# Seven block products instead of eight for the gates and ups of the second feed-forward, with one shared pool of equal tiles

## Chip, cores and metric

The kernel runs on one core of a Trainium2 chip. The metric is device time in microseconds (us) for one launch, the median of several runs. The engines are TensorE (PE, with its weight loads as PEld), VectorE (DVE), ScalarE (ACT), GpSimd (POOL) and SyncE (SP), whose queue issues nearly all the transfers.

## Reference

One layer of a hybrid bidirectional encoder over 768 real tokens (512 of one sequence, 256 of another) and 16 meta tokens, with rows of 1024 features:

```
h = h + 0.5 * swiglu(rmsnorm(h), ffn1 ...)                 # first feed-forward
u = rmsnorm(h);  proj = u @ w_in                           # q, k, v, z, xbc, dt
h = h + concat[diff_attention(q,k,v), ssd_mixer(z,xbc,dt)] @ w_out
h = h + 0.5 * swiglu(rmsnorm(h), ffn2 ...)                 # second feed-forward
y = rmsnorm(h), meta tokens dropped
swiglu(u, wg, wu, wd) = (silu(u @ wg) * (u @ wu)) @ wd      # wg, wu: 1024 x 2816, wd: 2816 x 1024
```

## Kernel before

All of h lives on chip with the features on the partitions: eight tiles of 128 features by the tokens. A float32 product is made of three products in float32r: each operand is split into a large part and a rest (`split`, L145: ScalarE casts the large part, VectorE subtracts it from the source for the rest), and `mm3` (L242) issues large x large, rest x large and large x rest (L246, L247, L248). `dense` runs `mm3` over the eight (or four) blocks of 128 features.

Weights come as blocks of 512 x 256 (512 KB) in the order of `plan`. `Weights.dma` loads a block into one of two buffers `wr`, `Weights.split` splits it into one of four buffers `wh` (large parts) and four `wl` (rests), and `done`, called after each product, allows the next split once a product's weights are used up (`NHL = 4` split blocks at a time). A raw buffer is free again when both parts of its block are made.

The second feed-forward, `ffn(2, ...)`, works on pairs of 128 hidden features, 11 pairs in all, in two halves of 384 tokens. For each pair, `gate_up` makes the gates (silu on ScalarE, L381) and then the ups (multiplied with the gates on VectorE, L390, and split for the last product): 2 weights x 2 rows of 128 x 2 halves, each one `dense` of eight blocks, 24 matmuls of 384 columns. `down` adds the product of a group of pairs with its part of `wd` to h (L410). The groups are `BOUNDS = [0, 1, 3, 5, 7, 9, 11]`: the first holds one pair, the others two, and the down product of a group is issued after the first pair of the next group.

The norm ahead of it, `nf = Norm(...)`, follows the last part of the output projection (`o_unit`, part 3), half by half. Its `chain` is a generator on the agenda: each `done` runs one step of it, and `nf.get(hf)` issues all that is left before the first product of that half. It makes 1/rms (`tok_rstd`), spreads it over the partitions (`bcast`), and for each of eight blocks scales h (L317) and splits it into rows `u`.

Memory on chip is in tagged pools: `u`, 16 tiles of 784 columns for split rows; `w3`, 16 tiles of 804 columns; `w4`, 15 tiles of 1056 columns; the weights' buffers; small ones. PSUM has three tags: `mm` and `x`, two banks each, and `S`, two pairs of banks. A tile is given a buffer of its tag when one is free. In the mixer stage each row of z and of the queries is gathered in a `w3` tile (written by L1041, two halves) and stored to DRAM by L1044.

Of the kernel before, what the change touches and what calls it, by code (L numbers as in the profile page):

```python
# [14 lines left out]
P = 128  # L15
# [32 lines left out]
def body(tc, x_prompt, x_sample, meta_tokens, ffn1_norm_w, ffn1_w_gate, ffn1_w_up, ffn1_w_down,  # L48
# [10 lines left out]
    up = top.enter_context(tc.tile_pool(name="up", bufs=1))  # L59
    wk = top.enter_context(tc.tile_pool(name="wk", bufs=1))  # L60
    sm = top.enter_context(tc.tile_pool(name="sm", bufs=1))
# [4 lines left out]
    def row_u():  # L66
        return up.tile([P, T1], F32R, tag="u", name="rowu", bufs=16)

    def w4(n=1056, dt=F32):
        return wk.tile([P, 1056], dt, tag="w4", name="w4", bufs=15)[:, :n]  # L70

    def w3(n=XW + 1, dt=F32):
        return wk.tile([P, XW + 1], dt, tag="w3", name="w3", bufs=16)[:, :n]
# [23 lines left out]
    # Silu's table, before the first data are there  # L97
# [10 lines left out]
    plan = []  # L108

    def plan_w8(key, src, c0, ncol=256):  # L110
        plan.extend(((key, 0), src, 0, 4, c0, ncol) if i == 0 else ((key, 4), src, 4, 4, c0, ncol) for i in range(2))
# [10 lines left out]
    def plan_down(f, wd, g):  # L122
        k0, k1 = 2 * BOUNDS[g], 2 * BOUNDS[g + 1]
        for cp in range(KD // 2):
            plan.append(((f, "d", g, cp), wd, k0, k1 - k0, cp * 256, 256))
# [15 lines left out]
    for part, k0 in enumerate(OUT_K):  # L141
        for cp in range(4):
            plan.append((("o", part, cp), w_out0, k0, 4, 256 * cp, 256))
    plan_ffn(2, ffn2_w_gate[0], ffn2_w_up[0], ffn2_w_down[0])
# [13 lines left out]
    NRAW, NHL = 2, 4  # L158

    class Weights:  # L160
        raw, ready = {}, {}
        n_dma = n_split = n_got = n_free = 0

        def dma(self):
            if self.n_dma >= len(plan):
                return
            key, src, k0, nk, c0, ncol = plan[self.n_dma]
# [11 lines left out]
        def split(self):  # L179
            j = self.n_split  # L180
            while self.n_dma <= j:
                self.dma()
            key, _, _, nk, _, ncol = plan[j]
            raw = self.raw.pop(j)
            hi = wp.tile([P, 4, 256], F32R, tag="wh", name="wh", bufs=NHL)
            lo = wp.tile([P, 4, 256], F32R, tag="wl", name="wl", bufs=NHL)
            ins = split(hi[:, :nk, :ncol], lo[:, :nk, :ncol], raw[:, :nk, :ncol])
            if ncol == 32:
                V.tensor_copy(hi[:, :nk, 32:64], lo[:, :nk, :32].bitcast(F32))
            self.ready[key] = [(hi[:, i, :], lo[:, i, :]) for i in range(nk)]  # L190
            self.n_split += 1
            while self.n_dma < max(self.n_split, 2) + NRAW and self.n_dma < len(plan):
                self.dma()
            return ins

        def pump(self, most=1):
            while most and self.n_split < min(len(plan), self.n_free + NHL):
# [3 lines left out]
        def get(self, key):  # L201
            assert plan[self.n_got][0] == key, (plan[self.n_got][0], key)
# [20 lines left out]
    def done(free=0):  # L223
        """A dense product has been issued: the next weights, then a step of what goes on beside it."""
# [6 lines left out]
    def complete(gen):  # L231
        """All of gen is issued by now."""
# [11 lines left out]
    def mm3(ps, a, b, start, stop):  # L244
        (ah, al), (bh, bl) = a, b
        nc.tensor.matmul(ps, ah, bh, start=start, stop=False)  # L246
        nc.tensor.matmul(ps, al, bh, start=False, stop=False)  # L247
        last_mm[0] = nc.tensor.matmul(ps, ah, bl, start=False, stop=stop)  # L248
# [9 lines left out]
    def rsqrt(v, name):  # L258
        """1/sqrt of a small tile of positive numbers: a first guess from the bits, then Newton's steps."""
# [11 lines left out]
    def diags(r, tiles):  # L271
        """diag(r[:n, j]) for each of tiles (j, n)."""
# [5 lines left out]
    def bcast(dst, dg, tiles):  # L278
        """dst's columns get the diagonals of dg, the same on each partition."""
# [7 lines left out]
    def add_sq(h, m, sums):  # L287
        """The squares of row m; the last row's are added to the others' sum by tok_rstd."""
        if m == 0:
            sums.append(w3(h.shape[-1]))  # L290
            S.activation(sums[0], h, AF.Square)
        elif m < KD - 1:
            sq = w3(h.shape[-1])
            S.activation(sq, h, AF.Square)
            G.tensor_tensor(sums[0], sums[0], sq, ALU.add)
        else:
            sums.append(w3(h.shape[-1]))
# [14 lines left out]
    def make_u(h, w, r_bc, c0, c1, u, ks):  # L312
        """u = the normed rows, columns c0..c1, split; r_bc starts at c0."""
# [9 lines left out]
    class Norm:  # L323
        """Follows the last additions to h, one half of the tokens at a time."""
# [14 lines left out]
        def get(self, hf):  # L339
            """The split rows, good for a half (or, without one, whole)."""  # L340
# [19 lines left out]
    def ffn(f, h, halves, u, after, first=None, last=None, rms=None):  # L360
        """first, last: other parts of the tokens for the first gates and the last sums; rms: 1/rms, if u is without."""
# [77 lines left out]

    h_d = dram.tile([KD, P, T2], F32, name="h_d")  # L440
# [27 lines left out]
    # the first norm's 1/rms, which the products with the gates get afterwards  # L468
# [9 lines left out]
    def put_h(eng, j, ps, c, n):  # L478
        """One engine to a tile of PSUM."""
# [8 lines left out]
    def squares(tiles):  # L488
        """Sums of squares by token; the squares themselves go nowhere."""
# [8 lines left out]
    def first_norm(tiles, ss):  # L498
        """1/rms of some of the tokens."""
# [9 lines left out]
    def take_x(b, ins):  # L509
        """Two tiles of tokens; ins: what their work on each engine stays behind."""  # L510
# [69 lines left out]
    o = 0  # L580
# [793 lines left out]
```

## Time and profile before

| | |
|---|---|
| three runs, us | 1911.4, 1912.8, 1915.61 (median 1912.8) |
| span of the profiled execution, us | 1908.7 |
| median less that span, us | 4.1 |
| TensorE busy | 1865.3 us (98%) |
| VectorE busy | 1012.4 us (53%) |
| ScalarE busy | 699.2 us (37%) |
| GpSimd busy | 97.0 us (5%) |
| mean granted clock of TensorE | 0.991 |

Spans run from the first to the last instruction. Matmuls are pipelined, so the duration of one overlaps the next; the distance between starts says what a matmul takes of TensorE's time. A granted clock of 1.00 is 2.4 GHz, of 0.50 is 1.2 GHz. The second feed-forward with the final norm runs from about 1331 us to the end.

### The profile page before, as it was taken

The numbers are of one execution on the slowest core, as the hardware profiler recorded it, in microseconds if no ns is written. First come the engines' busy times: TensorE is split into PE (matmuls) and PEld (weight loads), VectorE is DVE, ScalarE is ACT, GpSimd is POOL, SyncE is SP. The second block draws the span as 40 slices with busy tenths as digits, with TensorE's granted clock in tenths as the row PEclk, the third lists the DMA queues.
The fourth block names the chain that finished last, engine by engine and source line by source line (L and its number), as shares of the span: only waits on it lengthen the run. The fifth ranks groups of instructions, "written<-read, shape, count | busy, mean of one in ns | idle before, by whom it ended". The sixth has DMA issues, their size and how long they took to land.

```text
span 1908.7 us, 27592 instructions
## 1 busy us (share of the span) xinstructions
PE 1865.3 (98%) x11174; PEld 1798.8 (94%) x11174; DVE 1012.4 (53%) x2025; ACT 699.2 (37%) x1410; POOL 97.0 (5%) x118
## 2 busy tenths in 40 slices
PE   8999999999999999999899999999999999999998
PEld 7999999999998997888898998999999999999997
DVE  6444343344437498667788787666542424232333
ACT  6222121212123353678467675433322121222224
POOL 0000000000012000224100000002000000000002
PEclk9999999999998999999999999999899999999999
DMA  4242221222112232888432225321121212122111
GB/s 136 61 165 69 65 66 46 66 67 67 57 54 92 69 85 77 228 219 210 147 94 83 73 82 195 104 78 45 56 78 59 63 56 77 56 67 67 58 53 67
DMA packets 161266, 169.77 MB, mean 89 GB/s; under 512 B 9921, under 2 KB 146234, under 8 KB 161138
## 3 DMA queue, kind: packets, MB, share of 16 engines
q1 hardware_dynamic: 161122, 168.00, 28.7%
q8 instruction: 88, 1.44, 0.3%
q14 instruction: 40, 0.33, 0.1%
q10 hardware_dynamic: 16, 0.00, 0.0%
HBM read 148.54 MB, written 22.87 MB: 90 GB/s over the span
## 4 chain that ended last, share of the span: by engine, by line
PE 86%; DVE 7%; ACT 3%; DMA 1%; issue 1%; POOL 0%; SPq 0%; POOLq 0%; DVEq 0%; ACTq 0%
PE ps_mm L248 15%; PE ps_mm L247 15%; PE ps_mm L246 15%; PE ps_x L246 11%; PE ps_x L248 11%; PE ps_x L247 11%; DVE w L726 2%; PE ps_s L1162 2%; PE ps_s L1280 1%; DMA w<-ar_d 1%; ACT w L909 1%; DVE wl L148 1%; PE ps_s L841 1%; DVE w L1072 1%; DVE w L1182 1%
## 5 line engine op out<-in xcount | busy, mean ns | idle before, releaser
L248 PE MATMUL ps_mm<-rowu,wh 128*128 128x384 f32 (+3 forms) x1408 | 477.1, 339 | 4.8 <-DVE rowu L148 4.6
L246 PE MATMUL ps_mm<-rowu,wh 128*128 128x384 f32 (+3 forms) x1408 | 476.7, 339 | 4.6 <-DVE w L1041 2.0
L247 PE MATMUL ps_mm<-rowu,wl 128*128 128x384 f32 (+3 forms) x1408 | 475.9, 338 | 1.0 <-DVE wl L148 1.0
L148 DVE TENSOR_TENSOR wl<-wr,wh 128x1024 fp32r<-128x1024 f32 (+1 forms) x194 | 234.4, 1209 | 258.2 <-ACT wh L147 257.8
L147 ACT CAST wh<-wr 128x1024 fp32r<-128x1024 f32 (+1 forms) x194 | 198.4, 1024 | 391.0 <-PE ps_x L248 358.0
L247 PE MATMUL ps_x<-rowu,wl 128*128 128x392 f32 (+3 forms) x832 | 282.0, 339 | 0.0
L246 PE MATMUL ps_x<-rowu,wh 128*128 128x392 f32 (+3 forms) x832 | 281.9, 339 | 0.0
L248 PE MATMUL ps_x<-rowu,wh 128*128 128x392 f32 (+3 forms) x832 | 281.8, 339 | 0.0
L246 PEld LDWEIGHTS ps_mm<-rowu,wh 128*128 128x128 f32 x1408 | 266.0, 189 | 10.1 <-issue 2.7
L248 PEld LDWEIGHTS ps_mm<-rowu,wh 128*128 128x128 f32 x1408 | 265.6, 189 | 8.8 <-DVE rowu L148 6.4
L247 PEld LDWEIGHTS ps_mm<-rowu,wl 128*128 128x128 f32 x1408 | 265.9, 189 | 3.1 <-issue 1.4
L246 PEld LDWEIGHTS ps_x<-rowu,wh 128*128 128x128 f32 x832 | 158.5, 190 | 0.1
L247 PEld LDWEIGHTS ps_x<-rowu,wl 128*128 128x128 f32 x832 | 158.4, 190 | 0.0
L248 PEld LDWEIGHTS ps_x<-rowu,wh 128*128 128x128 f32 x832 | 158.1, 190 | 0.0
L147 ACT CAST w<-w 128x384 fp32r<-128x384 f32 (+4 forms) x106 | 59.0, 557 | 231.6 <-DVE w L390 228.5
L246 PE MATMUL ps_x<-w,wh 128*128 128x392 f32 (+3 forms) x352 | 119.7, 340 | 0.0
L246 PE MATMUL ps_mm<-w,wh 128*128 128x392 f32 (+3 forms) x352 | 119.5, 339 | 0.0
L248 PE MATMUL ps_mm<-w,wh 128*128 128x392 f32 (+3 forms) x352 | 119.4, 339 | 0.0
L248 PE MATMUL ps_x<-w,wh 128*128 128x392 f32 (+3 forms) x352 | 119.3, 339 | 0.0
L247 PE MATMUL ps_x<-w,wl 128*128 128x392 f32 (+3 forms) x352 | 119.0, 338 | 0.0
L247 PE MATMUL ps_mm<-w,wl 128*128 128x392 f32 (+3 forms) x352 | 118.8, 338 | 0.0
L410 DVE SCALAR_TENSOR_TENSOR w<-ps_x,w 128x392 f32<-128x392 f32 (+3 forms) x96 | 53.8, 561 | 113.1 <-PE ps_x L248 113.1
(286 smaller groups left out, 2587.8 us busy)
## 6 DMA issues: line engine op xcount, KB each, us to landing
wr<-in_ffn_w_gate_dram SPq DMA_DIRECT2D x44, 512.0 KB
wr<-in_ffn_w_up_dram SPq DMA_DIRECT2D x42, 512.0 KB
wr<-in_w_in_dram SPq DMA_DIRECT2D x42, 512.0 KB
wr<-in_ffn_w_down_dram SPq DMA_DIRECT2D x40, 512.0 KB
w<-ar_d SPq DMA_DIRECT2D x24, 512.0 KB
wr<-in_w_out_dram SPq DMA_DIRECT2D x16, 512.0 KB
w<-ar_d SPq DMA_DIRECT2D x24, 256.0 KB
w<-q_d SPq DMA_DIRECT2D x32, 192.0 KB
```

Of the source, the lines that this page charges most:

```text
L147: a = S.copy(hi, src)
L148: return a, V.tensor_tensor(lo, src, hi.bitcast(F32), ALU.subtract)
L246: nc.tensor.matmul(ps, ah, bh, start=start, stop=False)
L247: nc.tensor.matmul(ps, al, bh, start=False, stop=False)
L248: last_mm[0] = nc.tensor.matmul(ps, ah, bl, start=False, stop=stop)
L410: V.scalar_tensor_tensor(dst, ps[:, :n], 0.5, dst, ALU.mult, ALU.add)
L726: V.scalar_tensor_tensor(acc, pad[:, j:j + XW], prmT[:, cw:cw + 1], acc, ALU.mult, ALU.add)
L841: nc.tensor.matmul(ps[64 * d:64 * d + 64, g, :], B[:n, 64 * g:64 * g + 64], xd[:n, g * 512:(g + 1) * 512], start=True, stop=True)
L909: S.activation(ab[d][:, h, :], ab[d][:, h, :], AF.Exp, bias=ssm["asp"][:, c, col_s:col_s + 1])
L1072: V.tensor_tensor(dst[b], ps[a, s0:s1], dst[a].bitcast(F32), ALU.subtract)
L1162: nc.tensor.matmul(ps[:, b, :w], qh[c][part][:, P * i:P * i + P], kh[c][:, k0 + b * w:k0 + b * w + w], start=part == 0, stop=part == 1)
L1182: V.tensor_tensor_reduce(out=e[:, :nk].rearrange("p (b w) -> p b w", b=nb), in0=pss[c][:, :nb, :w], in1=tb[:, x0:x0 + nk].rearrange("p (b ...
```

## The change

**The product.** For pairs 1 to 10 of the second feed-forward, the gates (and likewise the ups) are one product of a 2 x 2 block matrix: weights 2 blocks of 512 features by 2 rows of 128 hidden features, tokens 2 blocks of 512 features by 2 halves of 384 tokens. It is computed with seven products of blocks (Winograd's form of Strassen's scheme) where there were eight, each of four `mm3`. Sums of weight blocks are made by VectorE in a buffer `sums` and split like weights: a split job of kind "a" takes one quarter of the pair's weights, "b" and "d" each two blocks that are sums, "c" two plain blocks. Sums of token blocks (`T`: t2, n1, m3, m4) are made once, at the end of the norm of the second half. The results are combined by VectorE, partly by accumulating two products in one PSUM bank (p2 onto p1, p3 onto p5, p4 onto p7). Pair 0 is computed as before.

**The order.** The seventh product of a quad (p4) is issued after the first product of the next one, and before the down product where a group ends. The down product of a group follows its own last pair. From the second group on it takes the second half of the tokens first.

**The memory.** `u` and `w3` become one pool of 31 tiles of 804 columns for the whole program. `w4` lies in a pool of its stretch: "mix" up to the last part of the output projection, "ffn2" after it (which has 18 tiles `f3` of 804 columns and `sums` in that place), "end" from the last down product on. Comments are gone.

```diff
+    def w3(n=XW + 1, dt=F32):
+        return wk.tile([P, XW + 1], dt, tag="w3", name="w3", bufs=31)[:, :n]
     def row_u():
-        return up.tile([P, T1], F32R, tag="u", name="rowu", bufs=16)
+        return w3(T1, F32R)
...
+        pool = st.enter_context(tc.tile_pool(name=name, bufs=1, reuse_waits="tile"))
...
+    def f3(n, dt=F32):
+        return stretch_pool[0].tile([P, XW + 1], dt, tag="f3", name="f3", bufs=18)[:, :n]
...
+    def plan_fast(key, src, c0):
+        a = len(raws_in)
+        for kind, r in (("a", (a,)), ("b", (a, a + 1)), ("c", (a + 1,)), ("d", (a, a + 1))):
+            jobs.append(((key, kind), kind, r))
+        raws_in.extend((src, k0, 4, c0, 256) for k0 in (0, 4))
...
+        def split_fast(self, key, kind, raw, hi, lo):
+            x, y = slice(0, P), slice(P, 2 * P)
+            if kind == "c":
+                ins = split(hi, lo, raw[0])
...
+            if kind == "a":
+                ins = split(hv[:, 0], lv[:, 0], raw[0][:, :, x])
+            else:
+                sums = stretch_pool[0].tile([P, 2 * 4 * P], F32, tag="sums", name="sums", bufs=1)
...
+                if kind == "b":
+                    V.tensor_tensor(t[:, 1], raw[0][:, :, y], raw[1][:, :, y], ALU.add)
+                    V.tensor_tensor(t[:, 0], t[:, 1], raw[0][:, :, x], ALU.add)
+                else:
+                    V.tensor_tensor(t[:, 0], raw[0][:, :, x], raw[0][:, :, y], ALU.add)
+                    V.tensor_tensor(t[:, 1], raw[1][:, :, x], raw[1][:, :, y], ALU.add)
+                    V.tensor_tensor(t[:, 1], t[:, 0], t[:, 1], ALU.add)
+                ins = split(hv, lv, t)
...
+    class FastNorm(Norm):
+        def chain(self, o, n, ss):
...
+            for k in range(KD):
+                hi, lo = two(row_u())
...
+                normed(t, k, o)
+                halves_of(hi, lo, t)
...
+            if not hf:
+                return
+            for k in range(4):
+                for i in range(2):
+                    normed(pairs[k][i][:, :n], k + 4 * i, 0)
+            yield 1
+            for k in range(4):
+                (t11, t12), (t21, t22) = (two(x) for x in pairs[k])
+                V.tensor_tensor(t12, t11, t12, ALU.subtract)
+                V.tensor_tensor(t22, t22, t12, ALU.add)
+                V.tensor_tensor(t11, t11, t22, ALU.subtract)
+                V.tensor_tensor(t21, t21, t22, ALU.subtract)
+                for i, (key, t) in enumerate((("t2", t22), ("n1", t12), ("m3", t11), ("m4", t21))):
+                    pair = two(f3(2 * n, F32R))
+                    halves_of(*pair, t)
+                    self.T.setdefault(key, []).append(pair)
...
+        def quad(which, pr):
...
+            def p1():
+                wget("a")
...
+                S2 = ps_s()
+                st["x"], st["y"] = S2[:, 0], S2[:, 1]
+                prod(st["x"], n0, st["a"][0], B[0][:4])
+                S.copy(at[m0, 0], st["x"][:, :n0])
+                done(1)
+            def p6():
+                wget("b")
+                prod(st["y"], n0, st["b"][0], T["t2"])
+                V.tensor_tensor(at[m1, 0], at[m0, 0], st["y"][:, :n0], ALU.subtract)
+                done()
+            def p5():
+                st["z"] = ps_mm()
+                prod(st["z"], n1, st["b"][1], T["n1"])
+                V.tensor_tensor(at[m1, 1], st["z"][:, :n1], at[m1, 0][:, :n1], ALU.add)
+                done(1)
+            def p2():
+                wget("c")
+                prod(st["x"], n0, st["c"][0], B[0][4:], True)
+                if which == 0:
+                    S.activation(at[m0, 0], st["x"][:, :n0], AF.Silu)
+                else:
+                    s = sg[m0][:, o0:o0 + n0]
+                    V.tensor_tensor(s, st["x"][:, :n0], s, ALU.mult)
+                    split_g(m0, o0, n0)
+                done()
+            def p7():
+                wget("d")
+                st["q"] = ps_x()
+                prod(st["q"], n0, st["d"][0], T["m3"])
+                V.tensor_tensor(at[m1, 1], st["q"][:, :n1], at[m1, 1], ALU.subtract)
+                out(m1, 1)
+                done()
+            def p3():
+                prod(st["z"], n1, st["d"][1], B[1][4:], True)
+                V.tensor_tensor(at[m0, 1], st["z"][:, :n1], at[m1, 0][:, :n1], ALU.add)
+                out(m0, 1)
+                done(1)
+            def p4():
+                prod(st["q"], n0, st["c"][1], T["m4"], True)
+                V.tensor_tensor(at[m1, 0], st["q"][:, :n0], at[m1, 0], ALU.subtract)
+                out(m1, 0)
+                done(1)
...
+        first()
+        norm.get(None)
+        down(0)
+        norm.B[1][:4] = [None] * 4
+        for g in range(1, len(BOUNDS) - 1):
+            late = None
+            for pr in range(BOUNDS[g], BOUNDS[g + 1]):
+                for which in range(2):
+                    steps = quad(which, pr)
+                    steps[0]()
+                    if late:
+                        late()
+                    for step in steps[1:6]:
+                        step()
+                    late = steps[6]
+            late()
+            if g == len(BOUNDS) - 2:
+                next_stretch("end")
+            down(g)
...
-    ffn(2, h2l, HALF2, nf.get, final, last=LAST)
+    ffn_fast(2, h2l, HALF2, nf, final, LAST)
```

`first()` computes pair 0 in the order of `gate_up(0)` before, asking `norm.get(i)` ahead of each product of half i. `out(m, hf)` applies the silu to a gate (ScalarE), or multiplies an up with its gate (VectorE) and splits it (a ScalarE cast and a VectorE subtraction).

## Rows read from the trace of the kernel before

**Rows 1.** The page's busy times: engine, us, share, instructions.
```profile
PE 1865.3 (98%) x11174; PEld 1798.8 (94%) x11174; DVE 1012.4 (53%) x2025; ACT 699.2 (37%) x1410; POOL 97.0 (5%) x118
```
**Rows 2.** Stretches: length, busy us (x count) of PE, PEld, DVE, ACT, POOL; clock; DMA.
```profile
1331.50:1375.00 43.50, 40.80 (x214) 39.67 (x214) 26.30 (x52) 16.29 (x29) 3.34 (x3) 0.88 0.16 49
...
1408.30:1425.20 16.90, 16.90 (x98) 16.90 (x97) 12.91 (x22) 4.30 (x6) 0.00 (x0) 1.00 0.43 131
1425.20:1862.00 436.80, 436.80 (x2508) 436.06 (x2506) 137.97 (x190) 89.63 (x125) 0.00 (x0) 1.00 0.20 63
...
1500.00:1600.00 100.00, 100.00 (x577) 100.00 (x576) 31.74 (x44) 20.16 (x28) 0.00 (x0) 1.00 0.21 64
```
**Rows 3.** Groups by form, 1400 to 1860: busy us, mean ns | idle before, releaser.
```profile
L148 DVE TENSOR_TENSOR wl<-wr,wh 128x1024 fp32r<-128x1024 f32 x55 | 67.4, 1225 | 155.2 <-ACT wh L147 155.2
L147 ACT CAST wh<-wr 128x1024 fp32r<-128x1024 f32 x56 | 58.7, 1049 | 161.5 <-PE ps_x L248 161.5
...
L148 DVE TENSOR_TENSOR w<-w,w 128x384 fp32r<-128x384 f32 x38 | 21.1, 556 | 16.8 <-ACT w L147 16.8
L147 ACT CAST w<-w 128x384 fp32r<-128x384 f32 x38 | 19.5, 512 | 102.9 <-DVE w L390 102.9
```
**Rows 4.** VectorE in order of time: start us, duration us, where others queue behind.
```profile
1335.63 0.54 DVE L1120 TENSOR_TENSOR w<-ps_mm,w 128x384 f32<-128x384 f32 x1
1336.10 0.54 DVE L148 TENSOR_TENSOR rowu<-w,rowu 128x384 fp32r<-128x384 f32 x1
...
1408.74 0.69 DVE L148 TENSOR_TENSOR wl<-wr,wh 128x512 fp32r<-128x512 f32 x1
1409.35 0.55 DVE L148 TENSOR_TENSOR w<-w,w 128x384 fp32r<-128x384 f32 x1
...
1413.79 1.22 DVE L148 TENSOR_TENSOR wl<-wr,wh 128x1024 fp32r<-128x1024 f32 x1
1414.92 0.55 DVE L410 SCALAR_TENSOR_TENSOR w<-ps_x,w 128x384 f32<-128x384 f32 x1
```
**Rows 5.** Stretches at the start of the second feed-forward, columns as rows 2.
```profile
1333.90:1338.40 4.50, 1.81 (x7) 0.94 (x6) 4.50 (x7) 1.30 (x3) 1.26 (x2) 0.88 0.37 118
1338.40:1347.40 9.00, 8.99 (x32) 8.88 (x33) 4.66 (x18) 1.77 (x2) 0.00 (x0) 0.50 0.20 60
```
**Rows 6.** TensorE in order of time, there.
```profile
1343.05 0.52 PE L248 MATMUL ps_x<-rowu,wh 128*128 128x384 f32 x1
1343.37 0.52 PE L246 MATMUL ps_x<-rowu,wh 128*128 128x384 f32 x1
```
**Rows 7.** ScalarE's casts of the first half's normed rows, in order of time.
```profile
1326.13 0.52 ACT L147 CAST rowu<-w 128x384 fp32r<-128x384 f32 x1 [0.89 <-DVE w L317]
...
1331.99 0.91 ACT L147 CAST rowu<-w 128x384 fp32r<-128x384 f32 x2
```
**Rows 8.** VectorE in order of time, second half of the norm and what follows.
```profile
1350.38 1.68 DVE L317 SCALAR_TENSOR_TENSOR w<-w,prmT,w 128x384 f32<-128x384 f32 x3 [4.89 <-ACT w L285]
...
1359.78 0.55 DVE L148 TENSOR_TENSOR w<-w,w 128x384 fp32r<-128x384 f32 x1
1365.44 1.23 DVE L148 TENSOR_TENSOR wl<-wr,wh 128x1024 fp32r<-128x1024 f32 x1 [5.12 <-ACT wh L147]
```
**Rows 9.** TensorE: first matmul after pair 0's last up.
```profile
1374.57 0.33 PE L246 MATMUL ps_mm<-rowu,wh 128*128 128x384 f32 x1
```
**Rows 10.** The issue of one 512 KB weight block on SP's queue.
```profile
1527.53 0.37 SPq L172 DMA_DIRECT2D wr<-in_ffn_w_gate_dram  x1
```
**Rows 11.** The stretch in which its bytes move, columns as rows 2.
```profile
1528.40:1530.60 2.20, 2.20 (x15) 2.20 (x14) 0.00 (x0) 0.49 (x1) 0.00 (x0) 1.00 0.79 236
```
**Rows 12.** Mixer stage: VectorE fills query rows, in order of time.
```profile
869.53 0.56 DVE L1041 TENSOR_SCALAR w<-ps_mm 128x384 f32<-128x384 f32 x1 [1.11 <-PE ps_mm L248]
...
889.80 0.56 DVE L1041 TENSOR_SCALAR w<-ps_mm 128x384 f32<-128x384 f32 x1 [2.41 <-PE ps_mm L248]
```
**Rows 13.** The store of the first of them, on SP's queue.
```profile
881.06 0.90 SPq L1044 DMA_DIRECT2D q_d<-w  x1
```

More of the change, by code (lines that the diff above doesn't have):

```diff
@@ L180, in split @@
             j = self.n_split
-            while self.n_dma <= j:
+            key, kind, rs = jobs[j]
+            while self.n_dma <= max(rs):
                 self.dma()
-            key, _, _, nk, _, ncol = plan[j]
-            raw = self.raw.pop(j)
+            raw = [self.raw[r] for r in rs]
             hi = wp.tile([P, 4, 256], F32R, tag="wh", name="wh", bufs=NHL)
             lo = wp.tile([P, 4, 256], F32R, tag="wl", name="wl", bufs=NHL)
-            ins = split(hi[:, :nk, :ncol], lo[:, :nk, :ncol], raw[:, :nk, :ncol])
@@ L188, in split @@
-            if ncol == 32:
-                V.tensor_copy(hi[:, :nk, 32:64], lo[:, :nk, :32].bitcast(F32))
-            self.ready[key] = [(hi[:, i, :], lo[:, i, :]) for i in range(nk)]
+            if kind == "1":
+                _, _, nk, _, ncol = raws_in[rs[0]]
+                ins = split(hi[:, :nk, :ncol], lo[:, :nk, :ncol], raw[0][:, :nk, :ncol])
+                if ncol == 32:
+                    V.tensor_copy(hi[:, :nk, 32:64], lo[:, :nk, :32].bitcast(F32))
+                self.ready[key] = [(hi[:, i, :], lo[:, i, :]) for i in range(nk)]
+            else:
+                ins = self.split_fast(key, kind, raw, hi, lo)
@@ L191, in split @@
+            for r in rs:
+                if last_use[r] == j:
+                    del self.raw[r]
+                    self.n_used += 1
             self.n_split += 1
-            while self.n_dma < max(self.n_split, 2) + NRAW and self.n_dma < len(plan):
+            while self.n_dma < max(self.n_used, 2) + NRAW and self.n_dma < len(raws_in):
                 self.dma()
             return ins
+        def split_fast(self, key, kind, raw, hi, lo):
+            x, y = slice(0, P), slice(P, 2 * P)
+            if kind == "c":
+                ins = split(hi, lo, raw[0])
+                self.ready[key] = [[(hi[:, i, c], lo[:, i, c]) for i in range(4)] for c in (x, y)]
+                return ins
+            hv, lv = (t.rearrange("p a b -> p (a b)").rearrange("p (s k f) -> p s k f", s=2, k=4) for t in (hi, lo))
+            if kind == "a":
+                ins = split(hv[:, 0], lv[:, 0], raw[0][:, :, x])
+            else:
+                sums = stretch_pool[0].tile([P, 2 * 4 * P], F32, tag="sums", name="sums", bufs=1)
+                t = sums.rearrange("p (s k f) -> p s k f", s=2, k=4)
+                if kind == "b":
[6 more added lines that the diff above has]
+                ins = split(hv, lv, t)
+            self.ready[key] = [[(hv[:, q, i], lv[:, q, i]) for i in range(4)] for q in range(1 if kind == "a" else 2)]
+            return ins
@@ L196, in pump @@
         def pump(self, most=1):
-            while most and self.n_split < min(len(plan), self.n_free + NHL):
+            while most and self.n_split < min(len(jobs), self.n_free + NHL):
                 self.split()
@@ L242, in body, with mm3 @@
     last_mm = [None]
-    def mm3(ps, a, b, start, stop):
+    def mm3(ps, a, b, start, stop, onto=False):
         (ah, al), (bh, bl) = a, b
-        nc.tensor.matmul(ps, ah, bh, start=start, stop=False)
-        nc.tensor.matmul(ps, al, bh, start=False, stop=False)
-        last_mm[0] = nc.tensor.matmul(ps, ah, bl, start=False, stop=stop)
+        nc.tensor.matmul(ps, ah, bh, start=start, stop=False, skip_group_check=onto)
+        nc.tensor.matmul(ps, al, bh, start=False, stop=False, skip_group_check=onto)
+        last_mm[0] = nc.tensor.matmul(ps, ah, bl, start=False, stop=stop, skip_group_check=onto)
     def cut(pair, a, b):
@@ L285, in bcast, with add_sq @@
         S.copy(dst[:, :c], ps[:, :c])
-    def add_sq(h, m, sums):
+    def add_sq(h, m, sums, new=w3):
         if m == 0:
-            sums.append(w3(h.shape[-1]))
+            sums.append(new(h.shape[-1]))
             S.activation(sums[0], h, AF.Square)
         elif m < KD - 1:
-            sq = w3(h.shape[-1])
+            sq = new(h.shape[-1])
             S.activation(sq, h, AF.Square)
@@ L296, in add_sq @@
         else:
-            sums.append(w3(h.shape[-1]))
+            sums.append(new(h.shape[-1]))
             V.tensor_tensor(sums[1], h, h, ALU.mult)
@@ L1341, in finish @@
             yield 1
-    ffn(2, h2l, HALF2, nf.get, final, last=LAST)
+    ffn_fast(2, h2l, HALF2, nf, final, LAST)
     drain()
+    stretch.pop().close()
     top.close()
```

166 lines of the change are left out of this document (150 added, 16 removed).

## The prediction, on record before the changed kernel ran

> **What bounds the kernel now.** I read the page's busy times first: TensorE has 98% of the span, VectorE 53%, ScalarE 37% [rows 1]. A busy share is an average, so next come the stretches. From 1425.2 to 1862.0 us, where pairs 2 to 10 run, TensorE is busy in every microsecond at the full clock, while VectorE works 138.0 of 436.8 us and ScalarE 89.6 [rows 2]. There the time is the number of matmuls times their distance, and the reader should take that distance from counts, not from durations that overlap: 577 matmuls in 100 us are 0.1733 us each [rows 2]. No wait of TensorE stands between 1360 and 1860 us, so a removed matmul is worth its whole distance, as long as VectorE and ScalarE can follow. The one weak place is the start of this feed-forward, 1331.5 to 1375.0, with TensorE 40.8 of 43.5 us busy at a mean clock of 0.88 [rows 2]. That is where the change adds most.
>
> **Removed: matmuls.** A pair's gates (or ups) take 2 x 2 x 8 x 3 = 96 matmuls before and 7 x 4 x 3 = 84 after. Ten pairs, two weights: 20 x 12 = 240 fewer, x 0.1733 = **41.6 us**. A quad of seven products now takes 84 x 0.1733 = 14.56 us, one product 2.08.
>
> **Added: VectorE's work in the quads.** The price of an instruction in a queue is the distance of starts: 0.47 us for 384 columns, 0.61 for 512, 1.13 for 1024 [rows 4]. Weights of one quad: six additions of 512 columns at most (two for b, three for d, and the rest of a as the sixth) and three rests of 1024: 6 x 0.61 + 3 x 1.13 = 7.05. Results: a gate quad has five combinations, 2.35; an up quad five, four multiplications and four rests, 6.11. So a gate quad needs 9.4 us of VectorE, an up quad followed by another quad 13.2, both under 14.56. The last up quad of a group splits down weights in place of the next quad's: 6.11 + 4 x 1.13 = 10.6. The weights are made several products ahead (four split blocks), and an accumulation onto a bank read by VectorE (z: p5, then p3) comes 2 products, 4.2 us, later, so lateness of a few microseconds stays covered. I price the quads at 0; without that cover they cost what VectorE lacks, in the second rival.
>
> A rule that speaks against this is in the Trainium skill, page "VectorE: DVE Perf Modes", section "The DRAIN you can't avoid": the next operation does not start until the pipeline has emptied. By it each instruction would cost its whole duration. The trace disagrees: the second starts 0.47 us after a first that lasts 0.54 [rows 4].
>
> **ScalarE.** Per quad three and a half casts of 1024 columns, 3.5 x 1.05 = 3.7, and five pieces of 384 columns at 0.51 [rows 3] make 6.2 of 14.56: hidden.
>
> **Transfers.** The bytes are unchanged, but both raw buffers stay taken until the sums of kind d are made. These follow b's rests, which wait for p5: 8.3 + 1.05 + 1.13 + 1.8 = 12.3 us into a quad. One block is issued at 1527.53 and its bytes end at 1530.6, 3.1 us [rows 10, 11]; two take some 5.3. They have landed 3 us into the next quad and are first multiplied in the quad behind that, 11 us later. Cost 0; if VectorE were later than that, TensorE would wait for the excess.
>
> **Added: the token sums at the start.** This I expect to cost most. `norm.get(1)` issues the rest of the second half's chain before the first product of that half: eight scalings and, for four sets, four combinations and four rests, 40 instructions of 384 columns ahead of all later work on VectorE. Before, the second half's rows end at 1359.78 + 0.55 = 1360.3, and VectorE then idles 5.1 us [rows 8]. The scalings cost 0.56 each (three in 1.68 [rows 8]), the others 0.47: 4.5 + 15.0 = 19.5, so 1379.8, and up to 4 us more, since the four combinations of a set hang on each other and each rest on a cast. Behind them stand the rests of the first down weights and the second half's ups. Pair 0's last up ends at 1374.6 [rows 9]; then comes down(0), which used to stand behind pair 1 and its 33 us of products. Its first matmul needs that rest, 0.61 after the sums: 1380.4 to 1384. TensorE waits 5.8 to 9.8 us; I take 7.
>
> Such a wait has a second price. Before, TensorE idled 2.7 of 4.5 us, and the next 9.0 us ran at a granted clock of 0.50 (1.2 GHz) [rows 5], matmuls 0.32 us apart [rows 6]. Nine microseconds then hold 28 matmuls, which take 4.9 at 0.1733: 4.1 lost. Together **11 us**, bounds 0 (the ups come first after all) and 14. The sums themselves are first read by p6, 16 down units (96 matmuls, 16.6 us) and one product later, so they are not late twice.
>
> **Moved: the first half's rows.** The casts of blocks 4 to 7 waited until 1331.99, just after the output projection had let go of its `u` tiles; the cast before them was at 1326.13 [rows 7]. The 31 shared tiles hold what is live there (8 of h, 8 of the projection, 8 rows, some sums). VectorE is busy through that stretch anyway [rows 5], so I take only **2 us** gain, bounds 0 and 5 (no fall of the clock).
>
> **Moved: the down products.** At a group's end p4's result needs two VectorE steps, a cast and a rest: 3 x 0.556 + 0.512 = 2.2 us [rows 3]. In groups 1 to 4 the down product starts with the second half, reading p3's result after p4 and two blocks, 2.08 + 1.04 = 3.1 us. In the last group p4's own result is due after nine matmuls of up to 512 columns, about 2 us. I take **1.5 us** for all ends, bounds 0 and 5.
>
> **Moved: the pools.** One tile fewer in all, and the mixer has 15 where 16 were. There a query row is filled from 869.53, stored from 881.06 [rows 13] and the next but one begins at 889.80 [rows 12]: with two rows instead of three there is still time. I take 0, bounds -5 and +8, since the order in attention may shift too.
>
> **Sum.** 1908.7 - 41.6 + 11 - 2 + 1.5 = 1877.6 us of span; the median lay 4.1 above the profiled span, so **1882 us**.
>
> **Rivals.**
> *The sums are hidden.* If the second half's ups and the down weights slip between the sums, TensorE waits under 2 us and the clock stays: 1882 - 11 = 1871. For it: 5 us of idle VectorE at 1360 and more later [rows 8]. Against: the sums are issued first and are nearly always ready.
>
> *VectorE bounds the quads.* At whole durations an up quad takes 13 x 0.556 + 6 x 0.69 + 3 x 1.225 = 15.0 [rows 3, 4], and if the seven rests each wait 0.44 for their casts (16.8 us over 38 [rows 3]) with nothing between, 18.1: 3.5 too long. A gate quad at 11.9 gives back 2.7. Five such up quads cost 4 to 17.5, group ends 5 more: 9 to 22, about 1897. The page's rule named above belongs to this rival; by that rule alone, 0.5 us in each of five quads, the time would be 1884. Against: the distances in rows 4.
>
> *The pool costs.* The missing tile holds up a row or a head's loads: 8 us, 1890. Against: rows 12 and 13.
>
> *The clock falls again and again (slower).* If in each up quad a bank or a buffer is late once for as long as at 1334, TensorE idles 2.7 and loses 4.1 behind it, 6.8 us [rows 5, 6]. Ten times is 68: 1950. It ends slower than before from five such places on (five x 6.8 = 34 against the 31 gained). For it: an up quad leaves VectorE 1.4 us of slack. Against: two banks of each kind and weights made ahead. The Trainium skill, page "TensorE: Matmul & The Clock Gate", section "HAM oscillation — how this bites in real kernels", says that repeated idle gaps send the engine back to the low clock each time; the trace has that once [rows 5].
>
> **Chances and range.** Forecast (1874 to 1890) 0.52; sums hidden 0.20; VectorE bounds 0.14; pool 0.06; clock falls 0.08. The likeliest is 1882. A range of 1864 to 1902 takes in the first four but for the ends of the third and leaves out the last, about 0.85. Under 0.2% (3.8 us) a difference can't be told from none here. Slower gets the clock case, 0.08, and the far end of VectorE's and the pool's cases gives 0.03 to no change: faster 0.89, same 0.03, slower 0.08.
>
> **What would show it.** Right: 240 matmuls fewer; TensorE without waits inside quads at 0.173 us; one wait of 6 to 10 us near 1375, released by a VectorE rest of down weights, with half clock behind it; VectorE at 65 to 90% in the quads. Wrong: waits of TensorE on VectorE in every up quad, a granted clock under 1.00 between 1400 and 1820, or a shift of the feed-forward's start against 1331 by more than 5 us.

## The result, and the profile after

The changed kernel takes 1880.0 us (median; 1877.4 to 1887.5), the kernel before 1913.1 beside it: ratio 0.983, 95% interval 0.981 to 0.985, or 33 us less. The forecast was 1882, range 1864 to 1902. A later set of runs gave 1882.8 and 0.9845 (0.983 to 0.986). The profiled execution has a span of 1875.7 against 1908.7.

Busy times on the page after, to be held against [rows 1]:

```profile
PE 1825.0 (97%) x10934; PEld 1756.2 (94%) x10934; DVE 1175.6 (63%) x2305; ACT 748.2 (40%) x1486; POOL 93.8 (5%) x118
```

240 matmuls are gone. VectorE has 280 instructions more, and 163 us more work. The stretches, with the columns of [rows 2]:

```profile
1331.50:1375.00 43.50, 39.71 (x210) 37.94 (x208) 37.20 (x80) 18.81 (x38) 3.38 (x3) 0.92 0.05 13
1374.00:1378.40 4.40, 0.14 (x1) 0.00 (x0) 4.40 (x11) 1.49 (x4) 0.00 (x0) 0.75 0.00 0
1378.40:1387.40 9.00, 8.97 (x39) 8.97 (x40) 6.94 (x13) 2.83 (x5) 0.00 (x0) 0.74 0.53 163
...
1425.20:1800.00 374.80, 374.80 (x2142) 374.06 (x2141) 249.11 (x376) 118.28 (x165) 0.00 (x0) 1.00 0.23 69
1500.00:1600.00 100.00, 100.00 (x573) 99.82 (x572) 65.49 (x99) 32.79 (x46) 0.00 (x0) 1.00 0.25 73
```

TensorE is as full between 1425 and 1800 us as before, at the full clock, with VectorE now at 66%. But 100 us hold 573 matmuls, not 577: 0.1745 us each instead of 0.1733. All waits of TensorE from 1290 to 1840 us (us in total, times, longest) stand ahead of the quads:

```profile
PE ps_mm L317 <- DVE wl L183: 4.3, 1, 4.3
PE ps_x L376 <- POOL w L365: 1.7, 1, 1.7
PE ps_mm L316 <- ACT w L537: 0.7, 1, 0.7
PE ps_mm L318 <- DVE w L538: 0.6, 2, 0.4
```

The first is the one forecast. In order of time on TensorE (start us, duration us; in brackets the wait): pair 0 has ended and down(0) begins. The first two lines are the large x large products of its first two units, which need no rest; the third needs the first rest. [rows 9] is the same place before:

```profile
1373.63 0.34 PE L316 MATMUL ps_mm<-w,wh 128*128 128x384 f32 x1
1373.81 0.34 PE L316 MATMUL ps_x<-w,wh 128*128 128x384 f32 x1
1378.43 0.69 PE L317 MATMUL ps_mm<-w,wl 128*128 128x384 f32 x1 [4.29 <-DVE wl L183]
1378.92 0.52 PE L318 MATMUL ps_mm<-w,wh 128*128 128x384 f32 x1
1379.24 0.52 PE L316 MATMUL ps_mm<-w,wh 128*128 128x384 f32 x1
...
1383.07 0.34 PE L317 MATMUL ps_mm<-w,wl 128*128 128x384 f32 x1
1383.25 0.34 PE L318 MATMUL ps_mm<-w,wh 128*128 128x384 f32 x1
```

After the wait the matmuls stand 0.32 us apart until 1383.07, then 0.18. The 4.64 us hold 14, which take 2.45 at 0.175: 2.2 us lost, so the place costs 6.5. VectorE at the same time (L533 scales rows, L563 to L566 combine, L538 subtracts casts, L183 is a rest of weights):

```profile
1349.12 1.68 DVE L533 SCALAR_TENSOR_TENSOR f<-w,prmT,w 128x384 f32<-128x384 f32 x3 [4.16 <-ACT w L355]
...
1361.63 1.14 DVE L533 SCALAR_TENSOR_TENSOR f<-w,prmT,w 128x384 f32<-128x384 f32 x2
1362.69 1.02 DVE L563 TENSOR_TENSOR f<-f 128x384 f32<-128x384 f32 x2
...
1375.82 1.95 DVE L538 TENSOR_TENSOR f<-f,f 128x384 fp32r<-128x384 f32 x4
1377.69 0.68 DVE L183 TENSOR_TENSOR wl<-wr,wh 128x512 fp32r<-128x512 f32 x1
```

From 1349 on it has no gap until that rest is made. The down weights' rest is issued behind all 40 instructions of the sums, and TensorE starts 0.7 us after it begins. From pair 0's end to the start of the last down products, whose first matmul is the next line, the kernel now takes 452.2 us:

```profile
1825.80 0.39 PE L316 MATMUL ps_mm<-w,wh 128*128 128x512 f32 x1
```

Before, these products start at 1859.01, and the stretch takes 484.4. Everything ahead together is 0.9 us earlier, the tail 0.2 us longer. This stretch of each profiled execution is used below beside the medians: what happens ahead of pair 0's end doesn't enter it.

### The profile page after: what moved, and what is told of

The parts are those of the page before. It is cut to its first block, busy times and chain, and to the rows that moved or that the text cites. A ratio compares the mean times of both kernels' runs of the same rounds, so it can differ in the third digit from the quotient of the medians.

```text
span 1875.7 us, 27520 instructions
## 1 busy us (share of the span) xinstructions
PE 1825.0 (97%) x10934; PEld 1756.2 (94%) x10934; DVE 1175.6 (63%) x2305; ACT 748.2 (40%) x1486; POOL 93.8 (5%) x118
## 4 chain that ended last, share of the span: by engine, by line
PE 83%; DVE 10%; ACT 3%; issue 2%; DMA 2%; POOL 0%; SPq 0%; ACTq 0%; POOLq 0%; DVEq 0%
PE ps_mm L316 13%; PE ps_mm L317 13%; PE ps_mm L318 13%; PE ps_x L316 10%; PE ps_x L318 10%; PE ps_x L317 9%; PE ps_s L316 2%; PE ps_s L317 2%; PE ps_s L318 2%; DVE w L1026 2%; PE ps_s L1462 2%; DMA w<-ar_d 1%; PE ps_s L1580 1%; ACT w L1209 1%; DVE wl L183 1%
## 5 line engine op out<-in xcount | busy, mean ns | idle before, releaser
L316 PE MATMUL ps_mm<-w,wh 128*128 128x384 f32 (+4 forms) x1520 | 518.7, 341 | 4.0 <-DVE w L1341 1.9
L317 PE MATMUL ps_mm<-w,wl 128*128 128x384 f32 (+4 forms) x1520 | 515.5, 339 | 4.3 <-DVE wl L183 4.3
L318 PE MATMUL ps_mm<-w,wh 128*128 128x384 f32 (+4 forms) x1520 | 516.5, 340 | 2.8 <-DVE w L183 2.2
L316 PEld LDWEIGHTS ps_mm<-w,wh 128*128 128x128 f32 x1520 | 287.2, 189 | 10.7 <-issue 2.7
L316 PE MATMUL ps_x<-w,wh 128*128 128x392 f32 (+4 forms) x864 | 293.7, 340 | 0.9 <-ACT w L1107 0.9
L318 PEld LDWEIGHTS ps_mm<-w,wh 128*128 128x128 f32 x1520 | 287.1, 189 | 7.4 <-DVE w L183 3.3
L317 PEld LDWEIGHTS ps_mm<-w,wl 128*128 128x128 f32 x1520 | 287.3, 189 | 7.0 <-DVE wl L183 4.6
L317 PE MATMUL ps_x<-w,wl 128*128 128x392 f32 (+4 forms) x864 | 292.8, 339 | 0.0
L318 PE MATMUL ps_x<-w,wh 128*128 128x392 f32 (+4 forms) x864 | 292.3, 338 | 0.0
L183 DVE TENSOR_TENSOR wl<-wr,wh 128x1024 fp32r<-128x1024 f32 (+1 forms) x194 | 222.1, 1146 | 87.6 <-ACT wh L182 86.8
L316 PEld LDWEIGHTS ps_x<-w,wh 128*128 128x128 f32 x864 | 163.7, 189 | 2.1 <-ACT w L1107 1.2
L317 PEld LDWEIGHTS ps_x<-w,wl 128*128 128x128 f32 x864 | 163.8, 190 | 0.7
L318 PEld LDWEIGHTS ps_x<-w,wh 128*128 128x128 f32 x864 | 163.5, 189 | 0.7
L182 ACT CAST w<-w 128x392 fp32r<-128x392 f32 (+4 forms) x130 | 73.8, 570 | 202.4 <-DVE w L460 118.3
L183 DVE TENSOR_TENSOR w<-w,w 128x392 fp32r<-128x392 f32 (+4 forms) x130 | 83.4, 645 | 29.4 <-ACT w L182 28.5
L183 DVE TENSOR_TENSOR wl<-sums,wh 128x1024 fp32r<-128x1024 f32 x40 | 49.0, 1225 | 29.6 <-ACT wh L182 29.6
```

Of the source, the lines that this page charges most:

```text
L182: a = S.copy(hi, src)
L183: return a, V.tensor_tensor(lo, src, hi.bitcast(F32), ALU.subtract)
L316: nc.tensor.matmul(ps, ah, bh, start=start, stop=False, skip_group_check=onto)
L317: nc.tensor.matmul(ps, al, bh, start=False, stop=False, skip_group_check=onto)
```

## The experiments

Theory A: the gain is the number of matmuls, the quads are covered, and the loss is the sums of tokens at the start. Its rivals: the order or the pools pay; VectorE is the bound in the quads; the sums' wait has another cause.

**The pools alone.** `plan_ffn`, `Norm` and `ffn` again for the second feed-forward, the new pools kept:

```
-    plan_ffn_fast(2, ffn2_w_gate[0], ffn2_w_up[0], ffn2_w_down[0])
+    plan_ffn(2, ffn2_w_gate[0], ffn2_w_up[0], ffn2_w_down[0])
...
-    ffn_fast(2, h2l, HALF2, nf, final, LAST)
+    ffn(2, h2l, HALF2, nf.get, final, last=LAST)
```

> The changed kernel's tile pools (one pool of 31 equal tiles, one pool for each stretch) with the second feed-forward's eight products, its order and its norm as they were in the kernel before. Theory A (the 33 us come from the 240 matmuls that are gone, and the pools are worth nothing): 1909 to 1917 us, 11174 matmuls. Rival 1 (the pools free tiles earlier and give a good part of the gain): 1900 or less. Rival 2 (the pools cost time that the products earn back): 1920 or more.

1916.5 us, ratio 1.0013 (1.0004 to 1.0022): about 2.5 us slower, so the pools earn nothing. Where they cost shows in a stretch of 400 us, first of the kernel before, then of this one:

```profile
1400.00:1800.00 400.00, 400.00 (x2301) 400.00 (x2300) 132.75 (x187) 83.58 (x117) 0.00 (x0) 1.00 0.21 66
```
```profile
1400.00:1800.00 400.00, 400.00 (x2280) 400.00 (x2279) 131.92 (x185) 83.19 (x117) 0.00 (x0) 1.00 0.22 66
```

The same products in the same order without a wait, 21 fewer of them: 0.1754 us apart instead of 0.1738. Only the pools differ between the two kernels, so the place of the tiles is the likely reason; what about it makes the difference isn't shown. Ahead of it the pools give something back:

```profile
1331.50:1375.00 43.50, 40.51 (x231) 38.58 (x230) 27.83 (x56) 18.81 (x32) 6.44 (x4) 1.00 0.18 53
```

231 matmuls at a clock of 1.00 where [rows 2] have 214 at 0.88: with the old norm and the new pools the clock doesn't fall at the feed-forward's start.

**Eight products in the new order.** Plain units with `norm.B` instead of the quads, no sums:

```
-                    steps = quad(which, pr)
...
+                    ws = W.get8((f, "gu"[which], pr))
+                    for m in range(2):
+                        for i, (o, n) in enumerate(halves):
+                            ps = ps_any()
+                            dense(ps[:, :n], ws, m, norm.B[i], 0, n)
```

> The changed kernel with eight block products for every pair of the second feed-forward: its order (both pairs of a group, then the group's downs), its rows for each half and its pools stay, and no sums of tokens or weights are made; the rows of gates times ups lie in the stretch's pool, and the last stretch is not opened. Theory A (only the number of matmuls counts): between pair 0's end and the first down matmul there is no wait, the matmuls are 11174 again, and the time is 1908 to 1918 us. Rival (the new order of gates, ups and downs is what pays): 1895 or less.

1916.6 us, ratio 1.0022 (1.0011 to 1.0033). The stretch around pair 0's end, then the first matmul behind pair 0 and the first of the last down products:

```profile
1374.00:1378.40 4.40, 4.40 (x27) 4.40 (x26) 2.49 (x5) 1.73 (x3) 0.00 (x0) 1.00 0.18 46
```
```profile
1376.72 0.34 PE L317 MATMUL ps_mm<-f,wh 128*128 128x384 f32 x1
...
1864.76 0.39 PE L317 MATMUL ps_mm<-f,wh 128*128 128x512 f32 x1
```

The order pays nothing either. Without the sums there is no wait at 1374, and the stretch from pair 0's end takes 488.0 us.

**No sums of tokens.** The plain rows stand in for the four operands:

```
+            for key, v in (("t2", self.B[0][:4]), ("n1", self.B[1][4:]), ("m3", self.B[0][4:]), ("m4", self.B[0][:4])):
+                self.T[key] = v
```

> The changed kernel without its sums of tokens: the first half's second scalings, the 16 additions and subtractions and the 16 splits of the four token operands are left out, and the plain rows stand in for the four operands, so what the products compute is not the feed-forward. Matmuls, weights' sums and the rest stay. Theory A (the sums' price is the wait of 4.3 us for the first down weights and the half clock behind it, 2 us): 1872 to 1875 us, and the first down matmul follows pair 0's last up within 0.5 us. Rival 1 (the sums are hidden, and the wait has another cause, such as the late transfer of the down weights): 1878 to 1882 us with the wait still there. Rival 2 (the sums cost more than their wait, by holding back pair 0's products too): 1869 or less.

1875.8 us, ratio 0.9805 (0.9791 to 0.9819). No wait of TensorE from 1360 to 1860, and full stretches:

```profile
1374.00:1378.40 4.40, 4.40 (x27) 4.40 (x26) 2.00 (x4) 1.36 (x3) 0.00 (x0) 1.00 0.00 1
1378.40:1387.40 9.00, 9.00 (x53) 9.00 (x52) 6.67 (x13) 1.69 (x4) 0.00 (x0) 1.00 0.40 117
```

80 matmuls where the changed kernel has 40: 40 x 0.175 = 7.0 us in these stretches. The median fell by 4.2 only (7.0 against the later set of runs). From pair 0's end to the last downs the 6 us are there:

```profile
1377.98 0.34 PE L316 MATMUL ps_mm<-w,wh 128*128 128x384 f32 x1
...
1824.04 0.39 PE L316 MATMUL ps_mm<-w,wh 128*128 128x512 f32 x1
```

446.1 us where the changed kernel takes 452.2, and where eight products take 488.0: 6.1 us for the sums and 42.0 for the 240 matmuls, 0.175 each. But pair 0 ends 4.3 us later here, and 4.0 of them lie ahead of all that the edit touches: this norm's first sum of squares on TensorE starts at 1317.99 us, in the changed kernel at 1313.95. The mixer is where that was lost: between 800 and 850 us this execution has 351 matmuls, the changed kernel's 374.

**The sums later.** The chain ends with its rows; a generator of its own makes the sums in small steps, and `complete` comes behind `down(0)`:

```
+            self.tail = self.sums(n, pairs, two, normed, halves_of)
+            later(self.tail)
...
         down(0)
+        complete(norm.tail)
```

> The changed kernel with the sums of tokens taken out of the second half's chain: the chain ends with its rows, and the sums are made in small steps behind pair 0's last products and beside the first group's down products; what is left of them is made before the first quad. Theory A (VectorE has room for them until the first quad's second product, and the only fault is that they stand in VectorE's queue ahead of the ups' multiplications and the down weights' rests): 1873 to 1876 us, no wait at the first down matmul. Rival (VectorE is full there, so that the wait only goes to the first quad's second product, which reads the first sums): 1878 to 1882 us with a wait of some 4 us at the first product that reads a token sum.

1874.7 us, ratio 0.9794 (0.9780 to 0.9808): the fastest version measured (the changed kernel's two sets: 0.9831 and 0.9845). The same two stretches, and VectorE:

```profile
1374.00:1378.40 4.40, 4.40 (x27) 4.40 (x26) 4.40 (x10) 2.38 (x6) 0.00 (x0) 1.00 0.11 16
1378.40:1387.40 9.00, 9.00 (x53) 9.00 (x52) 9.00 (x19) 1.96 (x5) 0.00 (x0) 1.00 0.36 109
```
```profile
1367.23 0.70 DVE L183 TENSOR_TENSOR wl<-wr,wh 128x512 fp32r<-128x512 f32 x1
```

The first rest of down weights stands at 1367.23 instead of 1377.69, the last split of the sums at 1392.39. The longest wait of TensorE from 1360 to 1860 is 0.4 us. VectorE had no less to do: it was the place in its queue that cost the time. From pair 0's end to the last downs it is 446.5 us, 5.7 less than in the changed kernel and 0.5 more than without the sums:

```profile
1376.78 0.34 PE L316 MATMUL ps_mm<-w,wh 128*128 128x384 f32 x1
...
1823.29 0.39 PE L316 MATMUL ps_mm<-w,wh 128*128 128x512 f32 x1
```

**More work for VectorE in the quads.** Additions nobody reads, three or eight per quad, spread behind its products:

```
+                        for _ in range(8 * (j + 1) // 5 - 8 * j // 5):
+                            V.tensor_tensor(idle, h[0][:, :n0], h[0][:, :n0], ALU.add)
```

> The changed kernel with three more additions of 384 columns on VectorE in each of the 20 quads, 60 in all, whose result nobody reads. At the measured start distance of 0.47 us they are 1.4 us of a quad's 14.7. Theory A (TensorE sets the quads' pace, and VectorE has some 13 us free in a group of four): +0 to +3 us against the changed kernel, no wait of TensorE within a quad. Rival (VectorE already sets the pace of the ups' quads): its work is added to the span, some +14 us over the ten ups' quads, or +28 over all twenty.

> The same with eight such additions in each quad, 3.8 us. Theory A: a group of four quads then holds 45.2 + 15.0 = 60.2 us of VectorE's work in 58.5 us, and an ups' quad 13.2 + 3.8 = 17 in 14.7; the buffers of PSUM can't carry 2.3 us, so waits of TensorE for VectorE stand in the ups' quads, and the time is 10 to 35 us longer than the changed kernel's. Rival 1 (VectorE is the bound already): +75 us, 160 additions at 0.47. Rival 2 (VectorE's busy time overstates its work, so that there is more room than the sum of busy time says): +5 or less.

Three: 1879.2 us, ratio 0.982 (0.980 to 0.984), no change. Eight, one run: 1887.6, but it isn't in the quads that the 8 us lie. First the changed kernel, then eight additions, over all quads and downs, and a group of four quads with the downs behind it:

```profile
1400.00:1830.00 430.00, 430.00 (x2451) 428.01 (x2450) 290.76 (x436) 139.86 (x196) 0.00 (x0) 1.00 0.24 70
```
```profile
1400.00:1830.00 430.00, 429.06 (x2449) 427.25 (x2448) 363.56 (x595) 138.65 (x193) 0.00 (x0) 1.00 0.24 70
...
1411.00:1470.00 59.00, 59.00 (x339) 58.86 (x338) 57.76 (x99) 24.11 (x34) 0.00 (x0) 1.00 0.27 81
1470.00:1503.00 33.00, 33.00 (x190) 32.76 (x189) 31.48 (x58) 4.79 (x6) 0.00 (x0) 1.00 0.17 49
```

2449 matmuls instead of 2451, with 73 us more on VectorE: TensorE waits 0.8 us in all. (The second execution is some 10 us later here, so the ends of this stretch hold other products; between 1400 and 1800 us the counts are 2285 and 2284.) My own 10 to 35 us missed. VectorE is at 98% in the quads and carries its lateness on into the downs, where it has room.

**Where the tiles start.** Tiles of 804 elements are laid 3232 bytes apart, so every second one starts 32 bytes behind a multiple of 64. One kernel puts all of them there, one none:

```
-        return wk.tile([P, XW + 1], dt, tag="w3", name="w3", bufs=31)[:, :n]
+        return wk.tile([P, XW + 13], dt, tag="w3", name="w3", bufs=31)[:, :n]
...
+    sm.tile([P, 8], F32, tag="shift", name="shift")
```

The last line is in the second alone; `f3` gets the same width in both.

> The changed kernel with the equal tiles (of the program's pool and of the stretch's) 816 elements wide instead of 804. In the kernel before, the rows of the second feed-forward lie in tiles that all start at a multiple of 64 bytes; in the changed one every second tile starts 32 bytes behind one, and in this one all do. Theory A (a matmul whose moving rows start 32 bytes off takes longer, which is why the kernel with the new pools alone lost some 4 us evenly over the second feed-forward): matmuls of the quads 0.1755 us apart or more instead of 0.1749, and +1 to +4 us against the changed kernel. Rival (the address is nothing, and the loss has another cause): within 1 us of the changed kernel.

> The same 816 wide tiles with 32 bytes put ahead of them, so that every one of them starts at a multiple of 64 bytes. Theory A: matmuls of the quads 0.1735 to 0.1742 us apart, and 2 to 5 us less than the changed kernel (1875 to 1878), 4 to 8 less than with all of them 32 off. Rival: within 1 us of both.

1883.1 us, ratio 0.9835 (0.982 to 0.985), and 1880.1, 0.9819 (0.9805 to 0.9834). The two in turn:

```profile
1400.00:1800.00 400.00, 399.53 (x2277) 398.46 (x2277) 267.08 (x404) 125.47 (x176) 0.00 (x0) 1.00 0.24 70
```
```profile
1400.00:1800.00 400.00, 400.00 (x2284) 399.02 (x2283) 267.29 (x403) 128.07 (x179) 0.00 (x0) 1.00 0.24 69
```

0.1757 us with all of them 32 off, 0.1751 with none; the changed kernel, half and half, has 2285 there, 0.1751 too. My theory falls: the offset is worth 0.0006 us a matmul at most, part of it the 0.5 us in which TensorE stood in the first of the two. Tiles at multiples of 64 bytes don't bring back the 0.1738 of before.

**Squares without GpSimd.** On top of the sums made later, rows 5 and 6 of each half go to TensorE's sum as tiles of their own:

```
+            if m < KD - 1:
+                S.activation(t, hs, AF.Square)
...
+            self.ss[hf].append(t)
```

> The kernel with the sums of tokens made later, and one thing more: the squares of rows 5 and 6 of each half are no longer added up by GpSimd but go to TensorE's column of ones as tiles of their own, 12 short matmuls more in all. Theory A (TensorE stands 1.7 us at the second half's first short matmul because GpSimd's last two additions end late, and runs at half clock for some 7 us behind it): no wait over 0.5 us there, no stretch at half clock between 1320 and 1400 us, and 3 to 5 us less than with the sums made later alone. Rival 1 (only the wait goes, the clock falls anyhow): 1 to 2 us less. Rival 2 (VectorE's last square or ScalarE's takes GpSimd's place as the last to come): within 0.5 us.

1877.7 us, ratio 0.982 (0.9805 to 0.984): 3 us more than with the sums made later alone, where theory A had 3 to 5 less and rival 1 had 1 to 2 less. (The edit adds 24 short matmuls, 10958 in all against 10934, not the 12 of the text above.) The wait of 1.7 us is gone, the half clock isn't. TensorE at the first half's short matmuls, then at the second half's:

```profile
1318.01 2.74 PE L376 MATMUL ps_x<-ones,w 128*128 128x1 f32 x24
...
1320.86 0.34 PE L317 MATMUL ps_x<-w,wl 128*128 128x384 f32 x1
1321.04 0.34 PE L318 MATMUL ps_x<-w,wh 128*128 128x384 f32 x1
...
1340.26 0.44 PE L318 MATMUL ps_mm<-w,wh 128*128 128x384 f32 x1 [0.39 <-DVE w L551]
1341.68 0.44 PE L316 MATMUL ps_mm<-w,wh 128*128 128x384 f32 x1 [0.98 <-ACT w L550]
...
1342.55 4.73 PE L376 MATMUL ps_x<-ones,w 128*128 128x1 f32 x24
...
1347.61 0.52 PE L317 MATMUL ps_x<-w,wl 128*128 128x384 f32 x1
1347.93 0.52 PE L318 MATMUL ps_x<-w,wh 128*128 128x384 f32 x1
```
```profile
1342.50:1343.00 0.50, 0.50 (x6) 0.50 (x5) 0.50 (x2) 0.50 (x1) 0.00 (x0) 0.96 0.00 0
1343.00:1343.50 0.50, 0.50 (x4) 0.50 (x4) 0.50 (x1) 0.50 (x1) 0.00 (x0) 0.50 0.00 0
```

What rival 1 says of the clock holds: it falls anyhow, and the matmuls behind stand 0.32 apart (1.2 GHz). The short matmuls alone don't do it: the same 24 take 2.74 us in the first half, and the matmuls behind them stand 0.18 apart. Ahead of the second 24, TensorE waited 0.4 and 1.0 us for rows; the clock is at half 0.5 us after they begin, and they take 4.73 us. Both groups had 12 before, which took 1.40 and 2.72 us: the edit adds 1.3 and 2.0 us of short matmuls, more than the wait that it removes.

**The last product in its place**, and the changed kernel once more beside it:

```
-                    if late:
-                        late()
-                    for step in steps[1:6]:
+                    for step in steps[1:]:
                         step()
-                    late = steps[6]
-            late()
```

> The changed kernel with each quad's last product made in its place, ahead of the next quad's first product instead of behind it. Theory A (the quads' products each find their operands ready long before, so the order across a quad's end is worth little): 0 to +3 us against the changed kernel. Rival (the last product's fresh accumulation needs that cover, and TensorE waits for VectorE or ScalarE at each of the 20 ends): +6 us or more, with waits at the quads' first or last product.

> The changed kernel as it is, beside the two others on the same chip. Theory A for all of it: 1876 to 1884 us, with the wait of 4.3 us for the first down weights. Rival (its first time was a lucky or unlucky set of runs): outside of this.

1883.6 us, ratio 0.985 (0.9835 to 0.986), against 1882.8, 0.9845 (0.983 to 0.986): the medians are within 1 us, as theory A had it, and again no wait at a quad is listed. Matmuls in 400 us:

```profile
1400.00:1800.00 400.00, 400.00 (x2276) 396.83 (x2275) 268.90 (x402) 124.28 (x174) 0.00 (x0) 1.00 0.23 69
```

The changed kernel's second set has 2287 there: 0.1749 us each against 0.1757 with the tiles in the same places. 17 of the distances here are 0.27 to 0.29 us, 4 in the changed kernel. From pair 0's end to the last downs it is 454.6 us against 453.0, so the late place of the last product earns some 1.6 us without any wait that shows. The changed kernel's second set has its wait of 4.3 us again. Its profiled execution took 1887.0 us, and most of the difference from the first lies in the mixer, which the change doesn't compute otherwise. The first set's execution, then the second's, with its wait:

```profile
842.00:852.00 10.00, 10.00 (x74) 8.38 (x73) 6.84 (x9) 7.45 (x12) 0.00 (x0) 1.00 0.38 117
```
```profile
PE ps_x L1222 <- DVE w L1214: 3.0, 1, 3.0
```
```profile
842.00:852.00 10.00, 10.00 (x56) 7.48 (x57) 4.99 (x8) 5.91 (x14) 0.52 (x1) 0.66 0.30 94
```

There one wait of 3.0 us (in the first set's execution two, of 0.7 at most) is followed by 0.66 of the clock. The run with eight additions has the same (clock 0.62). So the changed kernel's times spread over 10 us, and a few microseconds between two versions are better read from stretches than from medians.

## Why the prediction was right, step by step

- **Removed matmuls, -41.6.** Right: 42.0 us between eight products (488.0) and seven without the sums of tokens (446.1), from pair 0's end to the last downs.
- **VectorE's work in the quads, 0.** Right, and with more margin than the text gave it: not 1.4 us in an up quad but eight more additions in every quad were carried. The rival "VectorE bounds the quads" is dead, and "the clock falls again and again" with it: the clock is 1.00 from 1400 to 1800 us. The sums of tokens were not paid at whole durations either: the 32 combinations and rests from 1362.69 to 1377.77 took 15.1 us, 0.47 each, though one lasts 0.55. The Trainium skill's rule weighed there (page "VectorE: DVE Perf Modes", section "The DRAIN you can't avoid") was read as whole durations; the section goes on that a next operation which isn't held starts earlier, and with that the trace agrees.
- **Token sums, +11.** The mechanism, the place and the releaser were right, the size was not: 4.3 of wait and 2.2 of half clock, 6.5 by these lines and 6.1 against no_sums. The step that failed puts eight scalings behind the last row. In fact scalings and rows are mixed from 1349 on, and all of it ends at 1362.7, not at 1364.8. The up to 4 us for combinations that hang on each other, of which 1.2 were taken, didn't come. The second step, 4.1 us at half clock, was taken from a stretch of 9.0 us; here it lasted 4.6. "The sums are hidden" was wrong as a rival, but with the sums left out or made later the stretch is 6.1 and 5.7 us shorter.
- **First half's rows, -2.** Next to nothing came: from this norm's first sum of squares on TensorE to pair 0's end it was 60.0 us (1314.61 to 1374.57) and is 59.7 (1313.95 to 1373.63). The pools alone did keep the clock up there (231 matmuls, clock 1.00), and their stretch takes 57.1 (1316.41 to 1373.50): 2.9 less, not the bound of 5. In the changed kernel TensorE still waits 1.7 us for GpSimd and 1.3 for rows, and the clock falls.
- **Group ends, +1.5.** Not seen as waits. That the last product stands late earns 1.6 us; what the ends cost as they are wasn't measured apart.
- **Pools, 0.** Mis-sized, within its bounds. No row of the mixer is held up, as argued, but matmuls are further apart. From pair 0's end to the last downs the pools alone take 488.7 us and eight products in the new order 488.0, against 484.4 before: 4.2 and 3.6 us. Whether the pools have to do with the mixer's longer waits in some executions isn't shown.

With measured terms: 3.6 for pools and order, -42.0 for the products and 6.1 for the sums make -32.3 from pair 0's end to the last downs (484.4 to 452.2); 0.9 came off ahead of it and 0.2 was added behind: the span fell by 33.0. That the forecast was only 2 us off is partly luck: the sums were 4.9 us cheaper than their 11, and the pools with the ends 2.1 and the rows 1.1 dearer than written.

## What to carry to other kernels

Where TensorE is full and at its full clock, removed matmuls come off one for one, as long as other engines may lag a few products behind and catch up elsewhere: add their work over that whole stretch, not over one product. New preparatory work costs by its place in a queue, not by its sum: ask what stands behind it that another engine needs next, and cut it into steps that go between. Price a change of pools by the matmuls' distance too.

## What the runs showed of the hardware

- The distance of equal matmuls isn't fixed, though no wait is listed: over 400 us it was 0.1738 and 0.1754 us for the same products in two layouts of the tiles, and 0.1749 and 0.1757 in one layout with the last product of a quad in two places. What in the layout does it is open; the start modulo 64 bytes is not it.
- The clock fell to half 1.3 us behind waits of TensorE of only 0.4 and 1.0 us, while 24 short matmuls of one column ran; the same 24 matmuls without such waits ahead left it at 1.00. The Trainium skill (page "TensorE: Matmul & The Clock Gate", section "HAM oscillation — how this bites in real kernels") speaks of idle gaps; that agrees with the wait of 4.3 us here, behind which matmuls stood 0.32 us apart. Whether the short waits would do it without short matmuls behind them was not tried.
- A VectorE operation with no operand in PSUM takes longer when it starts beside a GpSimd addition. In the changed kernel L368 multiplies 384 columns; it took 0.56 us at 1312.63 with GpSimd idle, and 1.35 here. Three others of 384 columns that began beside an addition, at 1323.96, 1327.86 and 1332.08, took 1.37 to 1.38:

```profile
1336.75 2.35 POOL L365 TENSOR_TENSOR w<-w,w 128x384 f32<-128x384 f32 x2 [3.72 <-ACT w L364]
```
```profile
1336.90 1.35 DVE L368 TENSOR_TENSOR w<-w 128x384 f32<-128x384 f32 x1
```
